# Convolution, product and store of the last inner tile of a gated FFN written into the first chunk of the down projection

## Chip, cores and metric

The kernel runs on one core of a Trainium2 chip. The metric is the device time of one execution in microseconds; the median of 3 runs of the kernel before is 2664.31 us (2664.18 to 2665.32). Engines: TensorE (PE) multiplies matrices, VectorE (DVE), ScalarE (ACT) and GpSimd (POOL) work on elements, and SyncE (SP) issues most of the DMAs.

## The reference, cut to what matters

A decoder trunk of two layers on 1024 prompt tokens and 64 sample tokens, width 1024, all in float32. Each layer ends in a convolutional FFN:

```python
def conv_ffn(x, buf, w_up, conv_w, conv_b, w_down):
    h = x @ w_up                                  # 1024 -> 2 * 2816
    hp = jnp.concatenate([buf, h], axis=1)        # two rows of state ahead
    hc = conv_b + conv_w[0] * hp[:, 0:seq_len]
    for tap in range(1, 3):
        hc = hc + conv_w[tap] * hp[:, tap:tap + seq_len]
    gate, val = jnp.split(hc, 2, axis=-1)
    out = (jax.nn.gelu(gate) * val) @ w_down      # 2816 -> 1024
    return out, hp[:, -2:]                        # the last two rows are outputs too
```

## The kernel before

Every matrix product is done in three passes on a high and a low part of both operands (`mm3`, L815 to L817): a split is one ACT copy (L150) for the high part and one DVE subtraction (L151) for the low part.

The up projection, `ffn_up`, walks over 22 inner tiles `f` of 128 channels. Each has a gate half (s=0) and a value half (s=1). `inputs(f)` loads and splits the weights; `first(f)` and `rest(f, s)` are the products, whose results land in two buffers `hb` of tag `acc`. `conv(f, s)` is one ACT scaling with bias (L1198), two DVE taps (L1200), two small POOL copies of the last rows into `cvo` (L1203, L1204), and for the gate a GELU on ACT (L1206). `outputs(f)` multiplies gate and value on DVE (L1211) and stores the result to `gd` in DRAM (L1212). For odd `f` it also transposes the four pieces of `cvo` on PE (L1218), copies them into an 18-row buffer `cr` of tag `gr` (L1220) and stores that (L1223, L1224).

The down projection, `Down` and `ffn_down`, reads `gd` back. Its steps are (chunk, token tile) pairs. Chunk 0 takes inner tiles 0 and 1 in plain form: 9 steps k=0 to 8, the sample tile first, each with 12 products (8 for the sample tile) of L1426, evacuated by ACT (L1431). Chunk 1 and the following ones take four inner tiles each and pairs of token tiles by Strassen's scheme of seven products; their operands are differences that POOL makes (L1306 for weights, L1368 to L1371 for gated rows), their results are added by DVE (L1437). `stage(k)` loads the gated rows of step k (L1350 in chunk 0, L1354 for the sample tile, L1363 in the later chunks) and splits them. In chunk 0, step k is staged up to two steps ahead, and after each step two of 14 pieces of chunk 1's weights are prepared (`dn.load(1, 2)`). In layer 1 the last chunk is of Strassen's form, in layer 0 it is plain. The gated rows of inner tile 21, the last, are read by the last chunk only.

Buffers come from rings with a tag: 14 of `acc`, 5 of `gr`, 2 of `xr`, 2 of `raw`. The rows of steps 2 and 3 lie in `xr`, those of the other steps of chunk 0 in `gr`.

The order on each engine is not the order of the text. When the kernel is built, a planner plays the program with durations of its own and gives an engine, whenever it comes free there, the earliest-written instruction whose inputs and buffer are ready. Each engine and each DMA queue then executes its list strictly in that order. So a step that is written later loses to everything written before it that is ready at the same time, but it fills a hole if nothing else is ready.

Of the kernel before, what the change touches and what calls it, by code (L numbers as in the profile page):

```python
# [37 lines left out]
NF = FF // P  # L38
# [35 lines left out]
def trunk_kernel(ctx, tc, I, O):  # L74
# [19 lines left out]
    def psum_t():  # L94
        return psum("tr")
# [708 lines left out]
    def slot(tag, shape=None, dtype=F32):  # L804

        al = {"gx": "acc", "post": "acc", "junk": "gr"}
        shp, bufs = {"acc": ([P, 2 + SEQ + NB * 10], NACC), "gx": ([P, 4, 2 * P], NACC), "gr": ([P, 512], NGR),
                     "xr": ([P, D], 2), "junk": ([P, D], NGR), "post": ([P, D], NACC),
                     "cvo": ([P, 4, 18], 2), "cpar": ([P, 2 * NF, 20], 1), "ss": ([P, 1], 4)}[tag]
        tag = al.get(tag, tag)  # L810
        return pools["ph"].tile(shape or shp, dtype, tag=tag, name=nm(tag), bufs=bufs)
# [10 lines left out]
    def row_bcast(src):  # L822
        t = slot("post")
        nc.sync.dma_start(t, src.partition_broadcast(P))
        return t
# [272 lines left out]
    def ffn_up(i, down):  # L1098
# [8 lines left out]
        def inputs(f):  # L1107
            raws, hbs = [], []
            for s in range(2):
                raw = pools["w"].tile([P, 1024], F32, tag="raw", name=nm("raw"), bufs=2)  # L1110
                rv = u3(raw)
                nc.sync.dma_start(rv, wv[:, :, s * FF + f * P : s * FF + (f + 1) * P])
                raws.append(rv)
            a11, a12, a21, a22 = [r[:, 4 * k : 4 * k + 4] for r in raws for k in range(2)]
            s12, s34 = u3(slot("xr")), u3(slot("xr"))
            s1, s2, s3, s4 = [t[:, 4 * k : 4 * k + 4] for t in (s12, s34) for k in range(2)]
            V.tensor_tensor(s1, a21, a22, ALU.add)
            V.tensor_tensor(s2, s1, a11, ALU.subtract)
            V.tensor_tensor(s3, a11, a21, ALU.subtract)
            V.tensor_tensor(s4, a12, s2, ALU.subtract)  # L1120
            ws = []
            for r in (raws[0], s12, s34, raws[1]):
                hi, lo = u3(wslot("whi", F32R)), u3(wslot("wlo", F32R))
                split_evac(hi, lo, r)
                ws.append((hi, lo))
            for s in range(2):
                hb = slot("acc")
                hs = hb[:, 2 + SEQ :].rearrange("p (b r) -> p b r", r=10)
                GP.memset(hb[:, 0:2], 0.0)
                GP.tensor_copy(hs[:, :, 0:2], cp[:, s * NF + f, 4:NPAR].rearrange("p (b r) -> p b r", r=2))  # L1130
                hbs.append(hb)
            st[f] = ws, hbs, []
# [12 lines left out]
        def first(f):  # L1145


            (wg, w12, w34, wv_), (hg, hv), _ = st[f]
            lo, hi = slice(2, 2 + HT), slice(2 + HT, 2 + 2 * HT)
            p1, p2, p3 = psum(), psum(), psum()  # L1150
            v1, v2, v3 = [t[:, 0:HT] for t in (p1, p2, p3)]
            m1, u2, u3_ = hv[:, lo], hg[:, hi], hv[:, hi]
            prod(p1, wg, 0, x(0, 0), True)
            A.copy(m1, v1)  # L1154
            if f < NAHEAD:
                prod(p1, wg, 4, x(4, 0), False)
                A.copy(hg[:, lo], v1)
                yield
            prod(p2, w12, 4, lambda k: cb.rhs(0, k), True)
            V.tensor_tensor(u2, v2, m1, ALU.add)  # L1160
            prod(p3, w12, 0, x(0, HT), True)
            prod(p2, w34, 0, lambda k: cb.rhs(1, k), False)
            V.tensor_tensor(u3_, v2, m1, ALU.add)
            V.tensor_tensor(u3_, v3, u3_, ALU.add)
            if f >= NAHEAD:
                prod(p1, wg, 4, x(4, 0), False)
                A.copy(hg[:, lo], v1)
            prod(p3, w34, 4, x(4, HT), False)
            V.tensor_tensor(u2, v3, u2, ALU.add)  # L1169
            yield  # L1170
            prod(p2, wv_, 4, lambda k: cb.rhs(2, k), False)
            V.tensor_tensor(m1, v2, m1, ALU.add)
            yield
# [15 lines left out]
        def conv(f, s):  # L1189
            _, hbs, hcs = st[f]  # L1190
            if s == 0 and f % 2 == 0:
                cvos[f] = slot("cvo")
            cvo = cvos[f - f % 2]
            ft = s * NF + f
            hb = hbs[s]
            hs = hb[:, 2 + SEQ :].rearrange("p (b r) -> p b r", r=10)
            hc = slot("acc")[:, 0:TG]
            A.activation(hc, hb[:, 2 : 2 + TG], AF.Identity, bias=cp[:, ft, 3:4], scale=cp[:, ft, 2:3])  # L1198
            for tap in (1, 0):
                V.scalar_tensor_tensor(hc, hb[:, tap : tap + TG], cp[:, ft, tap : tap + 1], hc,  # L1200
                                       op0=ALU.mult, op1=ALU.add)
            co = cvo[:, 2 * s + f % 2]
            GP.tensor_copy(co[:, 0:2], hb[:, SEQ : SEQ + 2])  # L1203
            GP.tensor_copy(co[:, 2:NCV].rearrange("p (b r) -> p b r", r=2), hs[:, :, 8:10])  # L1204
            if s == 0:
                A.activation(hc, hc, AF.Gelu_apprx_tanh)  # L1206
            hcs.append(hc)

        def outputs(f):
            hcs = st.pop(f)[2]  # L1210
            V.tensor_tensor(hcs[1], hcs[0], hcs[1], ALU.mult)  # L1211
            nc.sync.dma_start(gd[f, :, 0:TG], hcs[1])  # L1212
            if f % 2 == 1:

                cvo = cvos.pop(f - 1)
                ps = psum_t()
                for j in range(4):
                    PE.transpose(ps[0:NCV, j * P : (j + 1) * P], cvo[:, j], ident)  # L1218
                cr = slot("gr")
                A.copy(cr[0:NCV], ps[0:NCV])  # L1220
                crv = cr.rearrange("r (s f) -> r s f", s=2)
                fs = slice((f - 1) * P, (f + 1) * P)
                nc.sync.dma_start(O["conv_prompt"][i, 0].rearrange("r (s f) -> r s f", s=2)[:, :, fs], crv[0:2])  # L1223
                nc.sync.dma_start(O["conv_sample"][i].rearrange("b r (s f) -> (b r) s f", s=2)[:, :, fs],  # L1224
                                    crv[2:NCV])
# [13 lines left out]
        for f in range(NAHEAD, NF):  # L1239
            inputs(f)  # L1240
            if f == NF - 1:
                down.begin()
            for s, _ in enumerate(first(f)):
                rest(f, s)
                conv(f, s)
            outputs(f)
        tail.combos = None


# [131 lines left out]
    def ffn_down(dn, i, xsrc, xdst, norm):  # L1381
# [5 lines left out]
        def fetch(j):  # L1387

            if not norm and j <= NTT:
                tt = ORDER[j]  # L1390
                r = slot("xr") if j % 2 else pools["w"].tile([P, 1024], F32, tag="raw", name=nm("raw"), bufs=2)
                nc.sync.dma_start(r[0 : tokens(tt)[1]], xsrc(tt))
                res[tt] = r
# [107 lines left out]
        def finish():  # L1501
            while ends:
                done(ends.pop(0))

        for k, (c, tt) in enumerate(dn.steps):
            kind, f0, nf = dn.plan[c]
            if c == nch - 1 and post[0] is None:
                post[0] = row_bcast(I["f_post_g"][i])
                for j in range(4):
                    fetch(j)  # L1510
            if kind == "p":
                dn.upto(k + 2)
                plain(k, c, tt)
                flush()
                if c == 0:
                    dn.load(1, 2)
            elif tt == NTT:
                sample(k, c)
                flush()
                dn.upto(k + 1)  # L1520
                finish()
            else:
                last = tt == 6
                g = pair(k, c, tt)
                for j in range(7):
                    if j == 2:
                        flush()
                        dn.upto(k + 1)
                        if not (norm is False and last):
                            finish()  # L1530
                    next(g)
                    if last and j != 2:
                        dn.load(c + 1, 1)
                if not last:
                    dn.load(c + 1, 1 if norm and c == nch - 2 else (3, 2, 2)[tt // 2])
                rest.append((g, c + 1 if last else nch))
            if c == nch - 1:
                ends += [tt] if kind == "p" or tt == NTT else [tt, tt + 1]
                if kind == "p":
                    finish()  # L1540
# [528 lines left out]
    down = Down(0)  # L2069
# [8 lines left out]
    down = Down(1)  # L2078
# [34 lines left out]
```

## Time and profile before

| what | value |
|---|---|
| median of 3 runs | 2664.31 us |
| profiled execution | 2665.99 us, of which the span is 2664.1 us |
| PE / DVE / ACT / POOL busy | 94% / 73% / 48% / 25% of the span |
| share of PE on the chain that ended last | 58% |
| passage from up to down projection, layer 0 | about 930 to 990 us from the span's start |
| the same, layer 1 | about 2385 to 2445 us |

A row of a timeline gives start, duration, engine, line, operation, tiles written and read, and in brackets how long the engine stood idle before it and what ended that. A busy PE is not PE at its peak, since the durations of matmuls overlap; distances between starts are safer. The granted clock (PEclk) is 1.00 at full speed.

### The profile page before, as it was taken

How to read it: one execution, taken by the hardware profiler on the slowest of the kernel's cores; microseconds unless marked ns; L12 is line 12 of the kernel's file. 1: busy time of each engine (PE TensorE's matmuls, PEld its weight loads, DVE VectorE, ACT ScalarE, POOL GpSimd, SP SyncE). 2: the span in 40 equal slices, each digit the busy share in tenths (PEclk: the TensorE clock that was granted, in tenths of full speed). 3: DMA queues.
4: the chain of work that ended last, by engine and by line, in shares of the span. 5: the costliest groups of instructions: out<-in, count | busy, mean ns of one | idle time of the engine just before them, and what ended most of it. 6: DMA issues, size and time to landing. Idle time of an engine off the chain costs nothing.

```text
span 2664.1 us, 39516 instructions
## 1 busy us (share of the span) xinstructions
PE 2493.7 (94%) x14234; PEld 2199.5 (83%) x14234; DVE 1947.8 (73%) x3543; ACT 1281.0 (48%) x2597; POOL 661.2 (25%) x1062
## 2 busy tenths in 40 slices
PE   3778998999999999999999899999899999998997
PEld 2777876999999977788777788877799999996776
DVE  7994358677777789984222688875877777778999
ACT  6763234444444454354322677764544444444433
POOL 3220030111111176501201222113011111127571
PEclk9999998999999999999999899999899999999999
DMA  5443233122222233445646333325322222233334
GB/s 144 104 97 88 84 126 126 58 76 78 85 72 78 81 117 97 125 134 183 207 158 210 104 83 96 98 93 173 127 69 79 75 75 74 75 98 105 92 107 154
DMA packets 265688, 286.77 MB, mean 108 GB/s; under 512 B 42268, under 2 KB 212564, under 8 KB 265492
## 3 DMA queue, kind: packets, MB, share of 16 engines
q1 hardware_dynamic: 261892, 273.55, 33.3%
q0 software_dynamic: 3088, 9.77, 1.7%
q8 instruction: 113, 1.85, 0.3%
q10 hardware_dynamic: 512, 0.92, 0.1%
q14 instruction: 83, 0.68, 0.1%
HBM read 193.58 MB, written 70.93 MB: 99 GB/s over the span
## 4 chain that ended last, share of the span: by engine, by line
PE 58%; DVE 13%; DMA 4%; issue 4%; ACT 3%; POOL 3%; SPq 0%; DVEq 0%; ACTq 0%; POOLq 0%
PE mm L815 17%; PE mm L817 17%; PE mm L816 17%; DVE acc L1437 2%; PE mm L1426 2%; DVE xT_lo L151 2%; DMA gr<-gd 2%; DVE S L1907 1%; ACT S L1911 1%; DVE xT_hi L151 1%; DVE wst L151 1%; PE mm L1935 1%; PE tr L876 1%; DVE acc L860 1%; POOL xr L1306 1%
## 5 line engine op out<-in xcount | busy, mean ns | idle before, releaser
L815 PE MATMUL mm<-xT_hi,whi 128*128 128x384 f32 (+1 forms) x1408 | 457.0, 325 | 2.0 <-ACT acc L1154 1.7
L816 PE MATMUL mm<-xT_lo,whi 128*128 128x384 f32 (+1 forms) x1408 | 456.2, 324 | 1.4 <-DVE xT_lo L151 1.4
L817 PE MATMUL mm<-xT_hi,wlo 128*128 128x384 f32 (+1 forms) x1408 | 454.0, 324 | 0.0
L815 PEld LDWEIGHTS mm<-xT_hi,whi 128*128 128x128 f32 x1408 | 265.4, 189 | 3.8 <-ACT acc L1154 2.4
L816 PEld LDWEIGHTS mm<-xT_lo,whi 128*128 128x128 f32 x1408 | 265.7, 189 | 2.2 <-DVE xT_lo L151 2.1
L817 PEld LDWEIGHTS mm<-xT_hi,wlo 128*128 128x128 f32 x1408 | 265.3, 189 | 0.8
L1203 POOL COPY cvo<-acc 128x2 f32<-128x2 f32 x88 | 54.2, 616 | 814.1 <-ACT acc L1186 814.0
L815 PE MATMUL mm<-whi,xT_hi 128*128 128x512 f32 x608 | 242.9, 404 | 5.8 <-ACT whi L798 5.8
L1200 DVE SCALAR_TENSOR_TENSOR acc<-acc,cpar,acc 128x1104 f32<-128x1104 f32 x176 | 239.9, 1385 | 4.7 <-ACT acc L1198 4.7
L816 PE MATMUL mm<-wlo,xT_hi 128*128 128x512 f32 x608 | 242.8, 400 | 0.1
L817 PE MATMUL mm<-whi,xT_lo 128*128 128x512 f32 x608 | 242.2, 400 | 0.0
L150 ACT CAST whi<-raw 128x1024 fp32r<-128x1024 f32 x88 | 92.7, 1053 | 248.5 <-PE mm L817 245.1
L1437 DVE TENSOR_TENSOR acc<-mm,acc 128x512 f32<-128x512 f32 x279 | 184.3, 679 | 8.4 <-PE mm L817 8.1
L151 DVE TENSOR_TENSOR wlo<-raw,whi 128x1024 fp32r<-128x1024 f32 x88 | 107.7, 1224 | 103.5 <-PE mm L816 90.8
L815 PE MATMUL mm<-acc,whi 128*128 128x384 f32 x528 | 178.8, 339 | 2.5 <-DVE acc L1160 2.5
L817 PE MATMUL mm<-acc,wlo 128*128 128x384 f32 x528 | 178.9, 339 | 0.0
L816 PE MATMUL mm<-acc,whi 128*128 128x384 f32 x528 | 178.3, 338 | 0.0
L815 PEld LDWEIGHTS mm<-whi,xT_hi 128*128 128x128 f32 x608 | 115.3, 190 | 36.9 <-ACT whi L798 6.2
L816 PEld LDWEIGHTS mm<-wlo,xT_hi 128*128 128x128 f32 x608 | 115.2, 189 | 27.9 <-DVE wlo L799 0.8
L817 PEld LDWEIGHTS mm<-whi,xT_lo 128*128 128x128 f32 x608 | 114.9, 189 | 27.9 <-issue 0.8
L1198 ACT ACTIVATE acc<-acc,cpar 128x1104 f32<-128x1104 f32 x88 | 114.2, 1313 | 18.1 <-DVE acc L1169 11.9
L1186 ACT COPY acc<-mm 128x256 f32<-128x256 f32 x88 | 32.4, 369 | 183.7 <-PE mm L817 183.7
(575 smaller groups left out, 6311.6 us busy)
## 6 DMA issues: line engine op xcount, KB each, us to landing
raw<-in_w_up_dram SPq DMA_DIRECT2D x88, 512.0 KB
gd<-acc SPq DMA_DIRECT2D x44, 552.0 KB
raw<-in_w_down_dram SPq DMA_DIRECT2D x44, 512.0 KB
gr<-gd SPq DMA_DIRECT2D x80, 256.0 KB
raw<-in_glu_w_dram SPq DMA_DIRECT2D x40, 256.0 KB
acc<-in_cache_k_dram SPq DMA_DIRECT2D x16, 512.0 KB
acc<-in_cache_v_dram SPq DMA_DIRECT2D x16, 512.0 KB
xj<-in_x_prompt_dram SPq DMA_DIRECT2D x8, 512.0 KB
```

The source lines that it names most:

```text
L150: A.copy(hi_ap, ps_ap)
L151: V.tensor_tensor(lo_ap, ps_ap, hi_ap.bitcast(F32), ALU.subtract)
L815: PE.matmul(out, lh, rh, start=start, stop=False, **kw)
L816: PE.matmul(out, lh, rl, start=False, stop=False, **kw)
L817: PE.matmul(out, ll, rh, start=False, stop=stop, **kw)
L860: V.scalar_tensor_tensor(y[:, hs], y[:, hs], r[0:n], xr[0:n, hs], op0=ALU.mult, op1=ALU.add)
L1186: A.copy(hb[:, 2 + n0 : 2 + SEQ], ps[:, 0:wp])
L1198: A.activation(hc, hb[:, 2 : 2 + TG], AF.Identity, bias=cp[:, ft, 3:4], scale=cp[:, ft, 2:3])
L1200: V.scalar_tensor_tensor(hc, hb[:, tap : tap + TG], cp[:, ft, tap : tap + 1], hc, op0=ALU.mult, op1=ALU.add)
L1203: GP.tensor_copy(co[:, 0:2], hb[:, SEQ : SEQ + 2])
L1426: PE.matmul(pa[h], lt, wt[:, h * 512 : (h + 1) * 512], start=st and j == 0, stop=sp and j == len(seq) - 1)
L1437: V.tensor_tensor(a, ps, a, ALU.add)
```

## The change

`conv(21, 0)`, `conv(21, 1)` and `outputs(21)`, 21 being the last inner tile, are no longer called at the end of `ffn_up`. They are left in a list, and `ffn_down` calls one of them after each of the steps k=3, 4 and 5 of chunk 0, behind that step's two pieces of weights. Both layers are changed alike.

```diff
@@ -1242,8 +1242,12 @@
                 down.begin()
             for s, _ in enumerate(first(f)):
                 rest(f, s)
-                conv(f, s)
-            outputs(f)
+                if f < NF - 1:
+                    conv(f, s)
+            if f < NF - 1:
+                outputs(f)
+
+        down.left = [lambda: conv(NF - 1, 0), lambda: conv(NF - 1, 1), lambda: outputs(NF - 1)]
         tail.combos = None
 
@@ -1514,6 +1518,8 @@
                 flush()
                 if c == 0:
                     dn.load(1, 2)
+                    if k >= 3 and dn.left:
+                        dn.left.pop(0)()
             elif tt == NTT:
```

## Rows read from the trace of the kernel before

**Rows 1.** The page's busy times: engine, us, share of the span, instructions.
```profile
PE 2493.7 (94%) x14234; PEld 2199.5 (83%) x14234; DVE 1947.8 (73%) x3543; ACT 1281.0 (48%) x2597; POOL 661.2 (25%) x1062
```
**Rows 2.** Layer 0 by stretches: us, busy PE, PEld, DVE, ACT, POOL, clock, DMA.
```profile
940.00:950.00 10.00, 8.02 (x36) 6.08 (x34) 10.00 (x8) 8.47 (x14) 8.07 (x4) 1.00 0.37 111
950.00:960.00 10.00, 6.41 (x17) 4.79 (x18) 9.03 (x13) 3.67 (x9) 5.55 (x2) 0.72 0.58 185
960.00:970.00 10.00, 10.00 (x42) 8.01 (x41) 6.57 (x10) 7.08 (x17) 8.64 (x11) 0.94 0.24 75
970.00:980.00 10.00, 9.49 (x41) 7.14 (x39) 8.34 (x15) 7.88 (x19) 9.46 (x16) 1.00 0.49 135
980.00:990.00 10.00, 9.43 (x39) 6.94 (x39) 9.32 (x15) 2.07 (x5) 6.92 (x8) 1.00 0.37 116
...
1010.00:1050.00 40.00, 39.14 (x167) 30.84 (x166) 38.05 (x59) 14.54 (x32) 26.41 (x36) 1.00 0.33 93
```
**Rows 3.** PE's waits from 920 to 985: for whom, us in total, times, longest.
```profile
PE mm L1426 <- ACT xT_lo L150: 3.5, 1, 3.5
PE mm L1426 <- DVE xT_lo L151: 2.1, 1, 2.1
```
**Rows 4.** PE's timeline, layer 0: chunk 0 and the start of chunk 1.
```profile
937.47 0.71 PE L1426 MATMUL mm<-whi,gr 128*128 128x512 f32 x2
...
947.62 0.40 PE L1426 MATMUL mm<-whi,xT_lo 128*128 128x512 f32 x1
951.52 1.22 PE L1426 MATMUL mm<-whi,xT_lo 128*128 128x512 f32 x2 [3.50 <-ACT xT_lo L150]
...
957.05 1.39 PE L1426 MATMUL mm<-whi,xT_lo 128*128 128x512 f32 x4 [2.07 <-DVE xT_lo L151]
...
970.83 0.39 PE L815 MATMUL mm<-wst,xT_lo 128*128 128x512 f32 x1
```
**Rows 5.** PE's timeline, layer 1: first products of chunk 0 and of chunk 1.
```profile
2392.10 0.71 PE L1426 MATMUL mm<-whi,gr 128*128 128x512 f32 x2
...
2425.82 0.39 PE L815 MATMUL mm<-wst,xT_lo 128*128 128x512 f32 x1
```
**Rows 6.** ACT's timeline, layer 0: the GELU, and the splits behind it.
```profile
946.58 1.13 ACT L1206 ACTIVATE acc<-acc 128x1104 f32<-128x1104 f32 x1 [1.20 <-DVE acc L1200]
...
951.07 0.71 ACT L150 CAST xT_lo<-gr 128x256 fp32r<-128x256 f32 x2
```
**Rows 7.** DVE's timeline, layer 0: two taps, and the next splits of gated rows.
```profile
944.14 4.74 DVE L1200 SCALAR_TENSOR_TENSOR acc<-acc,cpar,acc 128x1104 f32<-128x1104 f32 x2
...
956.58 1.09 DVE L151 TENSOR_TENSOR xT_lo<-gr,xT_lo 128x256 fp32r<-128x256 f32 x3
```
**Rows 8.** SP's timeline, layer 0: issues of loads and stores.
```profile
940.02 2.68 SPq L1350 DMA_DIRECT2D gr<-gd  x4
...
954.10 0.68 SPq L1223 DMA_DIRECT2D out_conv_prompt_dram<-gr  x1
...
957.82 0.38 SPq L1350 DMA_DIRECT2D gr<-gd  x1
958.29 15.51 SPq L1363 DMA_DIRECT2D gr<-gd  x6
```
**Rows 9.** The taps' line in the whole run: ns shortest, median, longest.
```profile
L1200 DVE SCALAR_TENSOR_TENSOR acc<-acc,cpar,acc x176: 1350/1361/2423, 478.7 to 2406.8; 128x1104 f32<-128x1104 f32 x176
```
**Rows 10.** POOL's timeline, layer 0: differences for weights, then for gated rows.
```profile
945.34 2.37 POOL L1306 TENSOR_TENSOR xr<-raw,raw 128x512 f32<-128x512 f32 x1
...
954.37 4.44 POOL L1306 TENSOR_TENSOR xr<-raw 128x512 f32<-128x512 f32 x1 [4.37 <-DVE xT_hi L151]
...
962.94 0.91 POOL L1368 TENSOR_TENSOR gr<-gr 128x128 f32<-128x128 f32 x1
```
**Rows 11.** Layer 1, a later stretch of the down projection; columns as in rows 2.
```profile
2490.00:2540.00 50.00, 49.55 (x214) 39.63 (x213) 48.68 (x80) 19.00 (x43) 33.12 (x45) 1.00 0.36 105
```
**Rows 12.** PE's waits from 2440 to the end: for whom, total, times, longest.
```profile
PE mm L815 <- DVE acc L1437: 5.8, 6, 2.6
```

## The prediction

> **What bounds the kernel now.** I read the page's list of busy times first [rows 1]: TensorE (PE) is busy 94% of 2664.1 us and VectorE (DVE) 73%, so a gain has to come from time in which PE stands or runs slowly, and DVE is the next to be full. Then I went to the one place that the change touches, the passage from the up projection into the down projection, which occurs once per layer, and cut it into stretches of 10 us [rows 2]. In layer 0 the reader sees PE busy 8.02 and 6.41 of 10 us from 940 to 960, a granted clock of 0.72 in the second, while DVE is at 10.00 and 9.03. PE's waits [rows 3] name two: 3.5 us for ACT and 2.1 us for DVE, both for a split of gated rows into `xT_lo`. PE's own timeline [rows 4] puts them in chunk 0 of the down projection: its first product starts at 937.47, PE waits before 951.52 and before 957.05, and chunk 1 starts at 970.83 (L815).
>
> Chunk 0 has 104 products (8 for the sample tile, 12 for each of 8 tiles). From 937.47 to 947.62 there are 44 of them without a wait: 10.15 us over 43 steps, 0.236 us each. So 104 x 0.236 = 24.5 us would do; it took 970.83 - 937.47 = 33.4 us. **8.9 us are lost in layer 0**: 3.5 + 2.1 of waiting and about 3.3 of products at a lower clock behind the waits. In layer 1 chunk 0 runs from 2392.10 to 2425.82 [rows 5]: 33.7 us, so 9.2 are lost. Together 18.1 us: no gain at this place can be more.
>
> Why does PE wait? The products of 951.52 are step k=4 (8 + 3 x 12 = 44 products lie before). Its split on ACT stands at 951.07, behind the GELU of the last inner tile, which itself waited for DVE [rows 6]. DVE at that time does that tile's convolution: two taps from 944.14 that took 4.74 us, and only at 956.58 come the next splits of gated rows [rows 7]. The other half of the cause is on SP [rows 8]: the loads of steps 4 to 7 go out together at 940.02, and the loads of step 8 (957.82) and of chunk 1 (from 958.29) stand behind the stores of `outputs(21)` (954.10 and following).
>
> **The change, part by part.** No instruction is added or removed: per layer, two ACT scalings, one GELU, four DVE taps (L1200, median 1.361 us, longest 2.423 [rows 9]), one DVE product, four small POOL copies, four PE transposes with one ACT copy, and three stores on SP are written later, after steps 3, 4 and 5.
>
> *What leaves chunk 0's front.* The splits of steps 4 and 5 and eight pieces of chunk 1's weights are now written before the first tap and win where both are ready. Also, `cr`, the 18-row buffer of `outputs(21)`, is of tag `gr`, and the loads of steps 4 to 7 took their buffers from the same tag after it. That four loads left SP back to back [rows 8], with their buffers not all due at one moment, I read as a plan that had to place `cr` first. Now `cr` comes after step 7's buffer, so the loads of steps 4 to 7 should go out earlier. I take both waits of rows 3 as gone, with the slow clock behind them: -8.9 us at PE if nothing else is late. From the other side it may be 0, if the planner fills the same free DVE time with the taps as now; they are long ready by then.
>
> *What is late next: DVE.* The taps still have to be done before chunk 1 is in full flow. DVE's idle time from 940 to 990 is 0 + 0.97 + 3.43 + 1.66 + 0.68 = 6.7 us [rows 2]. Work that is only moved can pull the rest forward by no more than this. In chunks that run well DVE is still idle 1.95 of 40 us (1010 to 1050), 2.4 us in 50. So 6.7 - 2.4 = 4.3 us are to be had, not 8.9.
>
> *What is late next: chunk 1's loads.* Steps 8 and 9 now take their `gr` buffers after `cr`, whose copy needs the transposes, written behind step 5: (8 + 5 x 12) x 0.236 = 16.0 us after the start, 953.5, and about 1 us for the transposes and the copy. The loads of chunk 1 would go out near 955, some 3.5 us sooner than at 958.29. From that load to chunk 1's first product it is 970.83 - 958.29 = 12.5 us now; if all of that is needed the start comes at 967.5, a gain of 3.3; if a part of it is slack, DVE's 4.3 decides. POOL has its share in these 12.5 us: it does differences for weights until 962.94 and only then the four differences of the first staged piece, of which the first took 0.91 us [rows 10].
>
> *The moved queues.* On SP the store of `gd` and the two of `cr` move past the loads of steps 4 to 7, a gain, and stay ahead of those of chunk 1. On ACT the GELU stays ahead of the evacuations of some later step of chunk 0; ACT waited 1.20 us at it [rows 6] and may again. On PE the transposes stand among the products; in the run before they cost no wait that the view of waits shows. The store of `gd` for f=21 is read by the last chunk only, far away. I set all this at 0, bounded by 1.2 either way per layer from the GELU's wait.
>
> *The port.* Two taps took 4.74 us, 2.37 each [rows 7], where the median is 1.361 [rows 9], while POOL worked on differences, of which one took 2.37 us [rows 10]: about 1.0 us lost by each tap. Of the four taps of this tile I see two paying it. Moved on, all four can: POOL is busy 8.64 and 9.46 of 10 us from 960 to 980 [rows 2], 5.55 and 8.07 earlier. That is 2 x 1.0 us more on DVE at most and 2 x 1.0 us less if none meets it; I take 0.
> The Trainium skill (SBUF — State Buffer, section "SBUF: two separate sides") speaks against the change here: VectorE operations with two SBUF inputs and GpSimd operations share a port pair that is locked for a whole instruction, and the other side blocks. The two rows of 2.37 us agree. By that rule alone every moved tap could hold POOL up for its full length, which would delay chunk 1 rather than start it earlier; that is the last rival below, priced there from rows: by the rule its 2672, by the rows the sum below.
>
> *Sum.* Layer 0: 8.9 from the waits, cut to 4.3 by DVE and to 3.3 to 4.3 by chunk 1's loads; I take 4. Layer 1 has the same geometry, but there DVE is busy 48.68 of 50 us further on [rows 11], and PE waits 5.8 us in all for its additions into `acc` [rows 12]; what is won at the start can partly be lost there. I take 3. Together 7 us. The profiled execution took 2665.99 us (its span of 2664.1 and 1.9 around it): 2665.99 - 7 = 2659.0. It lay 1.7 us above the median of 2664.31, so against that median **2657.3 us**.
>
> **The rivals.** What a measurement of this kernel tells from no change is about 0.2%, 5.3 us.
>
> *All of it is won (2646 to 2652).* If DVE's work gets shorter too, because taps no longer meet POOL (up to 2 us per layer) and the splits come in time, 12 to 18 us go. For it: the waits are plainly behind the taps. Against: DVE's 6.7 us of idle per passage.
>
> *Nothing happens (within 4 us, 2660 to 2668).* The planner hands DVE whatever is ready; the taps are ready soon after 940 and the weights' pieces wait for POOL (its difference of 2.37 us ends at 947.7 [rows 10]), so the taps would fall into the same hole as now. For it: from 940 to 950 DVE has no idle time, so whatever is ready runs. Against: the loads' order on SP should move all the same.
>
> *Slower (about 2672).* The mechanism is POOL's chain of differences for chunk 1, held up by the moved taps. Four taps of 1.36 us put in POOL's way are 5.4 us, and chunk 1's second product needs that chain. It decides from the point at which chunk 1's first L815 comes later than 33.4 us after the first L1426. With 1.4 us for the first product (6 x 0.236) as the only cover, chunk 1 is 4 us later in each layer: 2664.3 + 8 = 2672. For it: POOL at 8.64 and 9.46 of 10 us. Against: chunk 0 frees POOL's 4.37 us wait for DVE [rows 10] when weights are split sooner.
>
> **Chances.** The forecast (2653 to 2660.5, both layers gain 2 to 6 us) 0.46; all of it 0.10; nothing 0.24; slower 0.20. Of the forecast about 0.08 lies above 2659, within 0.2%, and the case of nothing lies there whole. That gives faster 0.38 + 0.10 = 0.48, same 0.08 + 0.24 = 0.32, slower 0.20. The range runs from 2648 (half of the case in which all is won) to 2670 (most of the case of nothing, a part of the slower one); the forecast's own range is 2653 to 2660.5.
>
> **What would show it.** In the changed profile: the loads L1350 of steps 4 to 7 issued before 940 relative to the same start (first L1426 at 937.5); no wait of PE before the 45th product; the granted clock at 1.00 through chunk 0; L1200 no longer between 944 and 952 but after the split of step 5; chunk 1's first L815 29 to 30 us after the first L1426 in both layers, and DVE idle under 4 us in the 50 us from the start of the passage. The prediction is wrong if the taps stand where they stood, if the loads of step 8 and chunk 1 come later than 20 us after the first L1426, or if a PE wait of more than 4 us shows up at chunk 1's first products on a POOL difference.

## The result and the profile after

The changed kernel takes 2675.58 us, median of 7 runs (2670.93 to 2680.25); the kernel before, beside it, 2664.31 us (2661.79 to 2668.01, 7 runs). The ratio is 1.0046, with a 95% interval of 1.0037 to 1.0056: the change makes the kernel **slower by 11.3 us**, where 2657.3 was forecast and 2670 was the end of the range. The profiled execution took 2676.99 us, its span 2675.2. Lines are shifted by four in the changed kernel: the plain products are L1430, ACT's evacuation L1435, DVE's additions into `acc` L1441, the loads of plain steps L1354, those of Strassen steps L1367.

The page's busy times, answering to [rows 1]: PE is busy 5 us less, DVE 10.5 us more, POOL 37 us less. (31.6 of POOL's 37 lie between the attention and chunk 0 of layer 1, in small copies that take less long; that stretch as a whole is 0.7 us longer.)
```profile
PE 2488.4 (93%) x14234; PEld 2194.6 (82%) x14234; DVE 1958.3 (73%) x3543; ACT 1278.3 (48%) x2597; POOL 624.1 (23%) x1062
```

**Chunk 0 did move.** PE's timeline in layer 0, answering to [rows 4], and in layer 1, to [rows 5]:
```profile
934.22 0.63 PE L1430 MATMUL mm<-whi,gr 128*128 128x512 f32 x2
...
958.86 1.75 PE L1430 MATMUL mm<-whi,xT_lo 128*128 128x512 f32 x4 [4.38 <-DVE xT_lo L151]
...
965.16 0.40 PE L815 MATMUL mm<-wst,xT_lo 128*128 128x512 f32 x1
...
2398.66 0.62 PE L1430 MATMUL mm<-whi,gr 128*128 128x512 f32 x2
...
2432.35 0.39 PE L815 MATMUL mm<-wst,xT_lo 128*128 128x512 f32 x1
```
The two waits of [rows 3] are gone from layer 0, and one of 4.38 us stands in a later step. Chunk 0 takes 965.16 - 934.22 = 30.9 us where it took 33.4; in layer 1 it takes 33.7 as before. The start itself is 3.3 us earlier than in the profile before, though the text up to there is the same; the twelve further kernels with that text start between 932.6 and 936.7, so that this is chance.

SP shows the loads early, as forecast (answers to [rows 8]):
```profile
897.03 4.28 SPq L1354 DMA_DIRECT2D gr<-gd  x3
...
928.79 0.38 SPq L1354 DMA_DIRECT2D gr<-gd  x1
...
939.36 0.38 SPq L1354 DMA_DIRECT2D gr<-gd  x1
944.52 0.33 SPq L1296 DMA_DIRECT2D raw<-in_w_down_dram  x1
944.94 0.67 SPq L1223 DMA_DIRECT2D out_conv_prompt_dram<-gr  x1
...
947.72 15.48 SPq L1367 DMA_DIRECT2D gr<-gd  x4
```
Three of the four loads that left together at 940.02 before, 2.6 us after chunk 0's start, now leave from 897.03 on, 37 us ahead of it. The last load of a step of chunk 0 leaves 5.1 us after chunk 0's start (before: 957.82 - 937.47 = 20.4 us), the first of chunk 1 at 13.5 (before 20.8).

**Where the time went.** On DVE, answering to [rows 7], the taps stand behind more splits, but in front of those that step 7 needs:
```profile
948.89 5.78 DVE L1200 SCALAR_TENSOR_TENSOR acc<-acc,cpar,acc 128x1104 f32<-128x1104 f32 x3 [0.26 <-ACT acc L1198]
954.59 1.74 DVE L151 TENSOR_TENSOR xT_lo<-raw,xT_lo 128x512 fp32r<-128x512 f32 x1
956.26 2.55 DVE L151 TENSOR_TENSOR xT_lo<-gr,xT_lo 128x256 fp32r<-128x256 f32 x3
```
Three taps take 1.93 us each on average, where the median is 1.361 [rows 9]; the split behind them takes 1.74 us, where the shortest of that size take 0.68. The taps are no longer than they were: all four take 7.3 us, before 7.5. What has grown is the splits. The windows of 50 us from the first product of chunk 0 (busy PE, PEld, DVE, ACT, POOL, then clock and DMA as in [rows 2]), first of the kernel before, then of the changed one:
```profile
937.47:987.47 50.00, 43.35 (x171) 33.01 (x169) 43.84 (x57) 30.57 (x66) 38.31 (x41) 0.93 0.44 134
```
```profile
934.22:984.22 50.00, 42.55 (x176) 32.54 (x175) 48.76 (x55) 31.24 (x64) 42.89 (x44) 0.97 0.40 122
```
This pair is the heart of the case. DVE's idle time fell from 6.2 to 1.2 us, as I had wanted it to, and DVE got through 55 instructions in place of 57. The idle time was filled by longer instructions (0.89 us each for 0.77): at the short length of each line and shape (5th percentile of both profiles) those that start in the 50 us would take 34.4 us, before 35.5, and what they take above it rose from 11.9 to 17.1. The clock rose as forecast from 0.93 to 0.97, and PE came only 3 products further (176 matmuls for 171, of which 4 and 1 are transposes).

Stretches that answer to those of [rows 2]:
```profile
950.00:960.00 10.00, 5.62 (x23) 3.94 (x22) 9.96 (x8) 7.46 (x15) 8.67 (x7) 0.96 0.14 43
960.00:970.00 10.00, 9.50 (x36) 7.28 (x34) 10.00 (x14) 6.46 (x15) 9.61 (x14) 0.87 0.41 134
970.00:980.00 10.00, 8.87 (x36) 6.61 (x36) 10.00 (x14) 3.39 (x8) 9.38 (x12) 1.00 0.60 175
...
1010.00:1050.00 40.00, 36.64 (x156) 28.82 (x155) 38.61 (x58) 13.18 (x30) 24.45 (x34) 1.00 0.28 84
```
From 960 to 980 DVE is at 10.00, where it had 6.57 and 8.34, and even from 1010 to 1050 PE makes 156 products where it made 167, at the full clock.

What chunk 0 won is lost again in chunks 1 to 4. PE's waits there in layer 0 (971 to 1142, and 965 to 1142), before and after:
```profile
PE mm L815 <- DVE acc L1437: 1.3, 3, 0.5
```
```profile
PE mm L815 <- DVE acc L1441: 8.7, 8, 1.9
```
In layer 1, from 2446 to the end, where [rows 12] has 5.8 us:
```profile
PE mm L815 <- DVE acc L1441: 10.1, 10, 2.6
```
PE waits until DVE has added an earlier product into `acc`. The additions themselves are no longer than before (0.676 us for 0.678 on average in layer 1); they come late, behind splits in DVE's list that are long. That the splits' length is the reason is put to the test in experiment 3.

Cut at the same products in every trace, the spans differ by these stretches (us; "excess" is my own working: over all DVE instructions from chunk 0 to the last chunk's first product in layer 0, to the end in layer 1, the time above the short ones, the 5th percentile, of the same line and shape):

| stretch | before | after | difference |
|---|---|---|---|
| start to chunk 0, layer 0 | 937.5 | 934.2 | -3.3 |
| layer 0: chunk 0 | 33.4 | 30.9 | -2.5 |
| layer 0: chunk 1 to the last plain chunk's end | 228.6 | 234.0 | +5.4 |
| layer 1, first part of the attention | 540.8 | 541.7 | +0.9 |
| end of the attention and start of its output projection (PE's instructions 9490 to 9890) | 79.5 | 84.7 | +5.2 |
| from there to chunk 0, layer 1 | 572.4 | 573.1 | +0.7 |
| layer 1: chunk 0 | 33.7 | 33.7 | 0.0 |
| layer 1: chunk 1 to the end | 238.3 | 242.9 | +4.6 |
| excess of DVE, layer 0 / layer 1 | 31.9 / 40.2 | 36.4 / 44.3 | +4.5 / +4.1 |

These are single executions, and the traces of the experiments below show how far they scatter. Where layer 0 is that of before (nine traces), the way from chunk 0 to the last plain chunk's end takes 260.9 to 262.4 us with an excess of 30.5 to 32.1. Where layer 1's text is that of before and POOL makes its differences (four traces), chunk 0 to the end takes 272.0 to 273.9 us with an excess of 39.7 to 40.2. Against that, layer 0's 264.9 us and its excess are clear of the scatter; of layer 1's 4.6 us it is 2.7.

Two things were to be explained: the loss behind chunk 0, and 5.2 us in the attention of layer 1, which the change does not touch.

### The profile page after: what moved, and what is told of

The parts are those of the page before. It is cut to its first block, busy times and chain, and to the rows that moved or that the text cites. A ratio compares the mean times of both kernels' runs of the same rounds, so it can differ in the third digit from the quotient of the medians.

```text
span 2675.2 us, 39551 instructions
## 1 busy us (share of the span) xinstructions
PE 2488.4 (93%) x14234; PEld 2194.6 (82%) x14234; DVE 1958.3 (73%) x3543; ACT 1278.3 (48%) x2597; POOL 624.1 (23%) x1062
## 5 line engine op out<-in xcount | busy, mean ns | idle before, releaser
L1203 POOL COPY cvo<-acc 128x2 f32<-128x2 f32 x88 | 48.2, 547 | 837.2 <-ACT acc L1186 837.2
L150 ACT CAST whi<-raw 128x1024 fp32r<-128x1024 f32 x88 | 92.4, 1050 | 280.5 <-PE mm L817 275.7
L1441 DVE TENSOR_TENSOR acc<-mm,acc 128x512 f32<-128x512 f32 x279 | 183.6, 677 | 9.0 <-PE mm L817 8.1
L817 PEld LDWEIGHTS mm<-whi,xT_lo 128*128 128x128 f32 x608 | 114.2, 188 | 27.5 <-issue 0.9
L1913 DVE CUSTOM_DVE_ANT_0 S<-mm,tb 128x512 f32<-128x512 f32 (+3 forms) x192 | 101.2, 551 | 21.0 <-PE mm L1911 17.5
```

Of the source, the lines that this page charges most:

```text
L150: A.copy(hi_ap, ps_ap)
L817: PE.matmul(out, ll, rh, start=False, stop=stop, **kw)
L1441: V.tensor_tensor(a, ps, a, ALU.add)
L1913: V.tensor_tensor_reduce(S_[j][:, k0 : k0 + w], ps[:, 0:w], H["tb"][:, b0 : b0 + w], 0.125, -3e38, ALU.add, ALU.max, mx[:, j, c : c + 1])
```

## The experiments

The theories, as the expectations name them: A, collisions of DVE's instructions with POOL's in the passages, and a new order of the lists at the end of the attention; B, that the loss in the attention is chance; C, that the earlier loads do the damage; D, that the moved work itself does; E, that the lists play no part; F, that POOL's work is too long, whatever it does. Medians stand beside those of the kernel before on the same chip.

**1. One layer at a time.** In `ffn_up` the tile is left over in one layer alone (`i != 1` for the other kernel):
```diff
-                if f < NF - 1:
+                if f < NF - 1 or i != 0:
                     conv(f, s)
-            if f < NF - 1:
+            if f < NF - 1 or i != 0:
                 outputs(f)
-        down.left = [...]
+        down.left = [...] if i == 0 else []
```


> The change in layer 0 alone. Theory A (each passage loses by itself, because moved taps make DVE's splits collide with POOL; and a change in layer 0 also makes the planner order the end of attention and the output projection anew): about +2.6 us in layer 0's passage and down projection, +6 us between 1725 and 1830 us, nothing in layer 1: +8 to +9 us in all, ratio 1.003. Theory B (what was lost near 1725 to 1830 is chance from run to run): +2 to +3 us, ratio 1.001. If the forecast holds in a layer by itself: -4 us.

Layer 0 alone: 2672.42 us against 2664.18, ratio 1.0031 (1.0020 to 1.0043), so +8.2 us.

> The change in layer 1 alone; the list of every engine is that of the kernel before up to layer 1's passage. Theory A: +4 us, all of it behind the first product of layer 1's chunk 0, nothing at the end of attention; ratio 1.0015. Theory B: the same +4, with the 6 us at the end of attention there or not by chance. If the forecast holds in a layer by itself: -3 us.

Layer 1 alone: 2666.77, ratio 1.0011 (1.0002 to 1.0020), +2.6 us; I had expected 4. The two add up to 10.8 of the 11.3 us. Layer 0's change carries most of it, and more than its own stretch shows: with layer 0 alone changed, that down projection (from chunk 0 to the last plain chunk's end) takes 263.0 us, where it took 262.0 before, and the attention's end 84.7 us again, where the kernel with layer 1 alone changed has 81.7. DVE's excess there is 34.0 us, with the same lists as in the changed kernel, which had 36.4. With layer 1 alone changed, layer 1's down projection takes 273.4 us with an excess of 40.4: no more than the unchanged ones. The traces thus do not show where the 2.6 us of layer 1 lie.

**2. The two halves of the change, in layer 1.** First only the 18-row buffer `cr`, its transposes and stores put off, so that the loads go out early while the taps stay; then only convolution, GELU, product and store of `gd` put off, so that the loads stay late:
```diff
+            if f < NF - 1 or i == 0:
+                last_rows(f)
+
+        def last_rows(f):
             if f % 2 == 1:
...
+        down.left = [lambda: None, lambda: None, lambda: last_rows(NF - 1)] if i == 1 else []
```


> Layer 1 alone; convolution, product and the store of gated rows stay where they were, only the transposes, the copy into the 18-row buffer and its two stores move behind step 5. Theory A (the buffer's place sets when the loads of steps 4 to 7 go out, the taps' place sets DVE's collisions): loads go out early, PE's first wait in chunk 0 shrinks, taps stay: 0 to -4 us. Rival C (early loads are what does the damage, since early splits crowd DVE before chunk 1): +2 to +4 us as with the whole change.

2663.72 us, ratio 0.9996 (0.9987 to 1.0005): no difference. The loads of steps 4 to 7 went out early, chunk 0 took 31.4 us, the whole down projection 271.3 (272.0 to 273.9 where it is unchanged). Early loads of chunk 0 do no harm, so C falls for them; they also win next to nothing. The first load of chunk 1 stayed at 20.9 us after chunk 0's start (before 20.0), so this run does not clear those.
```diff
-                conv(f, s)
-            outputs(f)
+                if f < NF - 1 or i == 0:
+                    conv(f, s)
+                else:
+                    rows(f, s)
+            if f < NF - 1 or i == 0:
+                outputs(f)
+            else:
+                last_rows(f)
+        down.left = [lambda: conv(NF - 1, 0), lambda: conv(NF - 1, 1), lambda: outputs(NF - 1)] if i == 1 else []
```


> Layer 1 alone; taps, GELU, product and the store of gated rows move, the last rows' copies, transposes and stores stay. Theory A: loads of steps 4 to 7 go out as before, so PE's wait in chunk 0 stays, and DVE's taps collide later: +3 to +6 us. Rival C: about 0.

2666.27 us, ratio 1.0007 (0.9998 to 1.0016). Against my expectation chunk 0 shrank, to 28.9 us, though the loads of steps 4 to 7 were late; the first of chunk 1 left at 13.5 us. The rest grew from 238.3 to 245.2. So the taps' place makes about half of chunk 0's loss of 9.2 us, and all of that gain is paid for behind it (274.1 us in all, 272.0 to 273.9 unchanged): PE's waits for additions from chunk 1 to the end come to 10.7 us in 11 places.

**3. POOL without its reads.** In layer 1's down projection POOL writes a constant where it made a difference:
```diff
+            self.diff = (lambda o, a, b, op: GP.memset(o, 0.01)) if i else GP.tensor_tensor
-                        GP.tensor_tensor(v[n], v[dif[n][0]], v[dif[n][1]], ALU.subtract)
+                        self.diff(v[n], v[dif[n][0]], v[dif[n][1]], ALU.subtract)
```
and the same for the four sums of gated rows. This once with the text's order of before, once with the taps of layer 1 put off, and once with the whole change in layer 1.

> Kernel before, but in layer 1's down projection POOL writes a constant where it formed differences of weights and of gated rows (these differences are left out), so POOL reads nothing from SBUF there. Control for the next one. Theory A (DVE's lengthened operations come from POOL's reads on the shared port): what DVE's operations in layer 1's passage and down projection take above their short durations falls from 38.8 us to under 10, and the stretch from chunk 0's first product to the end from 272.0 to 260 us or less. Rival D (DVE's durations vary for another reason, and DVE's plain work is the bound): excess stays above 25 us, the stretch within 4 us of 272.

> The same constants on POOL in layer 1, with the taps, GELU, product and store of layer 1's last inner tile moved and the last rows' part left in place. With POOL reading, that move shortened chunk 0 by 4.8 us and lost 6.9 us behind it. Theory A: without POOL's reads the gain of chunk 0 is kept or there is no loss to give back: 0 to 5 us shorter than the control. Rival D: chunk 1 and later still lose, 1 to 3 us longer than the control.

> The change in layer 1 as it is (all three calls behind steps 3 to 5), with constants written by POOL in layer 1's down projection in place of its differences (left out), to be held against the control without the change (stretch from chunk 0 to the end 253.8 us there, 272.0 and 273.4 to 276.6 with POOL's reads). Theory A (POOL's reads on the shared port make both the wait that the change was to remove and the loss behind it): 252 to 255 us, DVE's excess under 6 us, no difference to the control within 0.1%. Rival D (the moved work itself is what costs): 256 us or more.

Text of before: 2646.93 us, ratio 0.9940 (0.9922 to 0.9957). Taps put off: 2646.58, 0.9932 (0.9917 to 0.9947). Whole change: 2643.16, 0.9918 (0.9904 to 0.9933). Layer 1 takes 253.8, 253.2 and 253.4 us from chunk 0 to the end, for 272.0: some 18 us are gone, and with them the difference that the change makes there: the moved work by itself costs nothing, once POOL reads nothing, and D falls. PE's timeline of the first of the three:
```profile
2386.57 0.71 PE L1427 MATMUL mm<-whi,gr 128*128 128x512 f32 x2
...
2411.60 0.40 PE L815 MATMUL mm<-wst,xT_lo 128*128 128x512 f32 x1
```
Chunk 0 takes 25.0 us with the taps where they were in the text: about the 24.5 that I had worked out for a chunk without a wait. DVE's groups of the down projection in layer 1 (count, then busy us and mean ns of one, then its idle time before them), before:
```profile
L1437 DVE TENSOR_TENSOR acc<-mm,acc 128x512 f32<-128x512 f32 x155 | 102.3, 678 | 2.9 <-PE mm L817 2.9
L151 DVE TENSOR_TENSOR xT_lo<-gr,xT_lo 128x256 fp32r<-128x256 f32 (+2 forms) x53 | 34.5, 660 | 4.6 <-ACT xT_lo L150 3.0 <-PE mm L1426 1.4
```
after:
```profile
L151 DVE TENSOR_TENSOR xT_lo<-gr,xT_lo 128x256 fp32r<-128x256 f32 (+2 forms) x52 | 36.1, 708 | 3.3 <-ACT xT_lo L150 3.2
```
and with the text's order of before but POOL writing constants:
```profile
L1438 DVE TENSOR_TENSOR acc<-mm,acc 128x512 f32<-128x512 f32 x155 | 103.9, 687 | 18.8 <-PE mm L817 17.0 <-PE mm L1446 1.5
L151 DVE TENSOR_TENSOR xT_lo<-gr,xT_lo 128x256 fp32r<-128x256 f32 (+2 forms) x53 | 23.8, 461 | 6.5 <-ACT xT_lo L150 6.2
```
The same 53 splits take 461 ns for 660. DVE's excess in the stretch, 40.2 us by the definition above (38.8 in the expectation), falls to 3.8, and DVE, no longer late, now waits 17.0 us for PE before its additions. The additions stay as long as they were: one of their operands is a product in PSUM (`mm`), only the other lies in SBUF.

A constant is also written faster than a difference (POOL had 43 us of work in place of 159), so POOL's length was a rival. To tell the two apart, each constant was written three times:
```diff
-            self.diff = (lambda o, a, b, op: GP.memset(o, 0.01)) if i else GP.tensor_tensor
+            self.diff = (lambda o, a, b, op: [GP.memset(o, 0.01) for _ in range(3)]) if i else GP.tensor_tensor
```


> The kernel before, but in layer 1's down projection POOL writes a constant three times over where it made a difference (the differences are left out). In the run with one constant each POOL had 42.7 us of such work in that stretch (160 of 205 ns, 34 of 527 ns), against 159 us of differences; three each give 128 us, 3 x 205 = 615 ns where a difference of gated rows took 609 to 626. So POOL's chain is nearly as long as before, but reads nothing from SBUF. Theory A (what costs is that POOL's differences read SBUF beside DVE's splits): the stretch from layer 1's chunk 0 to the end stays at 253 to 257 us, the median at 2644 to 2651, and the splits into xT_lo at some 0.46 us. Rival F (what costs is POOL's length: chunk 1's operands come later, whatever POOL does meanwhile): the stretch goes back to 264 to 272 us, the median to 2657 to 2665, while the splits stay short.

2646.47 us against 2665.14, ratio 0.9932 (0.9909 to 0.9956); the stretch takes 253.2 us and chunk 0 24.4. A window of layer 1 in that trace, answering to [rows 11]:
```profile
2490.00:2540.00 50.00, 50.00 (x217) 40.47 (x216) 45.66 (x87) 22.51 (x49) 31.25 (x156) 1.00 0.39 110
```
POOL is busy 31.25 of 50 us, nearly the 33.12 of before, and PE stands at 50.00 all the same. F falls: it is not how long POOL works, but what it reads while DVE works. Two differences to the real kernel remain in all four. A constant does not wait for the load of its operands. And the planner, which plays the constants too, writes other lists: 101 of the 416 rows of DVE's list in that stretch stand elsewhere than before, and the taps run at 1.2 to 8.7 us after chunk 0's start where they ran at 3.5 to 14.7. The shorter splits are measured by themselves; how much of the 18 us comes from them and how much from these two is not shown. Layer 0, which carries most of the loss, had no such run.

**4. Layer 0's tile later or sooner.** The condition `k >= 3` in `ffn_down` becomes `k >= 6` or `k >= 1`, with layer 0 alone changed:
```diff
-                    if k >= 3 and dn.left:
+                    if k >= 6 and dn.left:
```


> Layer 0 alone, the three calls behind steps 6, 7 and 8 instead of 3, 4 and 5. In this version the planner's lists from the end of attention on are those of the kernel before. Theory A (the new lists there cost about 5 us): +1 to +4 us, from layer 0's passage alone, with 79 to 83 us for the end of attention. Theory B (that stretch varies by chance): the same as layer 0's change behind steps 3 to 5, +8.

> Layer 0 alone, the three calls behind steps 1, 2 and 3. Here the lists of layer 0's passage differ least from those of the kernel before, but those from the end of attention on are the other ones, as in the changed kernel. Theory A: +4 to +7 us, nearly all between the end of attention and the output projection. Theory B: 0 to +2 us.

With 6: 2666.86 us against 2664.96, ratio 1.0004 (0.9993 to 1.0014). With 1: 2670.49, 1.0020 (1.0011 to 1.0029). The planner's lists may explain the order of the two medians; the two profiled executions, at 2670.77 and 2669.64 us, do not show it. Compared row by row, the lists for layer 1's attention are those of before with 6, and are others with 1, as they are with 3: between the two down projections DVE's list differs at 267 places, 51 of them in this stretch, under a text that is the same. The stretch took 78.0 to 83.3 us in the eleven traces with the lists of before (mean 81.5) and 84.7, 84.7 and 87.1 in the three with the new lists (mean 85.5). That is 4.0 us, with no overlap, and E falls with it. With 1, layer 0's own down projection is the shortest of all, 259.5 us; the 5.6 us over the mean in the attention eat that up.

B is right for a part of the 5.2 us, and POOL and DVE show it at the start of the stretch, where the lists are still the same. Before, DVE's combination (L1921, starting at 1741.20) was ahead of POOL's subtraction, and POOL took the longer time:
```profile
1741.20 1.14 DVE L1921 SCALAR_TENSOR_TENSOR S<-S,cc,S 128x896 f32<-128x896 f32 x1
```
```profile
1741.78 2.81 POOL L1879 TENSOR_TENSOR kl<-qraw,kl 128x1024 fp32r<-128x1024 f32 x1 [5.21 <-ACT kl L1878]
```
After, POOL is ahead, and DVE takes 2.90 us for the same combination (L1927):
```profile
1742.84 2.90 DVE L1927 SCALAR_TENSOR_TENSOR S<-S,cc,S 128x896 f32<-128x896 f32 x1
```
```profile
1742.40 2.40 POOL L1885 TENSOR_TENSOR kl<-qraw,kl 128x1024 fp32r<-128x1024 f32 x1 [7.02 <-ACT kl L1884]
```
DVE ends when POOL has ended and its own 1 us is done (1742.40 + 2.40 + 0.94 = 1745.74). Which of the two starts first is not the change's doing: with the lists of before, DVE is first in three traces, where the stretch takes 78.0 to 79.6 us, and POOL is first in eight, where DVE takes 2.9 us and the stretch 81.3 to 83.3 (mean 82.4). The profile before is one of the three. With the new lists POOL is first in all three traces. So about 3 us (85.5 for 82.4) go with the new lists, and the rest of the 5.2 is who came first. What in the new lists costs the 3 us I have not shown.

**5. Both layers late, and layer 1 early.** The same condition with 6 in both layers, and with 1 in layer 1 alone:

> Both layers, the three calls behind steps 6 to 8 in place of 3 to 5; the lists between the layers are those of the kernel before. Theory A: chunk 0 shorter still (27 to 29 us), chunk 1 and later longer by more than that, +2 to +3 us in each layer, nothing at the end of attention: +3 to +6 us, about half of what the change cost. Rival E (the loss is set by how far the moved work gets into chunk 1, and the planner's lists elsewhere do not matter): +10 us or more.

> Layer 1 alone, the three calls behind steps 1 to 3: taps before most of chunk 0's later splits, the loads of steps 5 and later behind the 18-row buffer. In layer 0 this place gave 259.5 us from chunk 0's first product to the end of the last products, 2.5 less than before. Theory A (only the number of collisions counts): -2 to +1 us; if it is below the kernel before by its interval it is the version to take.

Both with 6: 2669.10 us against 2664.54, ratio 1.0016 (1.0007 to 1.0024), with the lists of before in the attention. Its chunk 0 takes 27.5 and 27.8 us, shorter by 5.9 and 6.0; the rest is longer, by 6.9 in layer 0 and by 9.8 in layer 1. Layer 1 alone with 1: 2661.88, ratio 0.9991 (0.9982 to 1.0000). That is the best of all, 2.7 us, at the edge of what the runs tell from nothing; its down projection took 269.4 us where it took 272.0.

Put side by side, layer 0 gives a series in the place of the tile (chunk 0, then chunks 1 to 4, up to the last chunk's first product, us): before 33.4 and 171.3; from k = 1 32.2 and 168.6; from k = 3 30.6 and 174.9 (layer 0 alone) or 30.9 and 176.5 (both); from k = 6 27.4 and 179.2 (layer 0 alone) or 27.5 and 178.1 (both). From 1 to 6 the later the tile comes, the shorter is chunk 0 and the longer what follows; from 1 to 3 that is longer by more, from 3 to 6 by more in one pair of traces (4.3 for 3.1 us) and by less in the other (1.6 for 3.4). The excess does not follow the place: 34.5 us with 1, 34.0 and 36.4 with 3, 33.5 and 33.8 with 6.

## Why the prediction was wrong

**Right:** that PE's waits in chunk 0 were to be had at all, and their size (24.5 us for a free chunk 0; 24.4 to 25.0 were measured in three of the four kernels of experiment 3; in the other, chunk 1's first products stand among those of chunk 0); that `cr` held back the loads, which did go out early; that DVE's idle time would fall below 4 us in the 50 us (1.2). **Half right:** the wait before the 45th product went, but another came in step 7; the clock of the second stretch rose from 0.72 to 0.96, not to 1.00, and sank to 0.87 in the third; chunk 1 came 30.9 us after chunk 0's start in layer 0, not 29 to 30, and in layer 1 it gained nothing.

**Wrong, the step that failed:** "So 6.7 - 2.4 = 4.3 us are to be had", with the term of the port set at 0. I took DVE's idle time as room into which work can be pulled forward, each instruction at its length of before. The idle time went, and it was filled by instructions that had become longer: 55 in 48.76 us for 57 in 43.84. The excess of DVE grew by 4.5 us in layer 0 and 4.1 in layer 1, and the waits for additions by 8.7 - 1.3 = 7.4 and 10.1 - 5.8 = 4.3 us. For the four taps the 0 was right, and the bound of 2 us held (7.3 us for 7.5 in layer 0, 6.6 for 7.5 in layer 1). But the splits of chunks 0 to 4 also stand beside POOL's differences, and for those the sum had no term; it ended at chunk 1's start, and for layer 0 counted what was won there as kept. In this pair of profiles the missing term is the 4 to 5 us of excess; with one layer changed alone it was 2 to 4 us in layer 0 (34.0 against 30.5 to 32.1) and nearly none in layer 1 (40.4 against 39.7 to 40.2), so that its size stays open. None of the prediction's three signs of being wrong showed: they all looked at chunk 0 and the start of chunk 1, and the loss came behind.

**Half wrong, the cause of the wait:** I read the waits as the taps' place in DVE's list. Their place is half of it (28.9 us when only taps, GELU and product moved). But with POOL's reads gone the taps may stay where they are in the text, and chunk 0 takes 25.0 us. The reading that fits is that the list was too long because its instructions were; since the planner's list changed too in that run, it is argued and not shown alone.

**Not seen:** that a change in layer 0 can re-order lists some 800 us later, in text that is the same. The prediction holds no term for it; it goes with some 3 to 4 of the 11.3 us. I had named the planner as what decides, but thought only of the queues beside the change.

**The rivals.** The slower one, 2672, was nearest in size, and its ground, the shared port, was right. Its mechanism was not: it decides, as written, from a chunk 1 that starts later than 33.4 us after chunk 0, and that came at 30.9 and 33.7; no wait of PE on a difference of POOL's shows there. What was held up was DVE by POOL, not POOL by DVE. "Nothing happens" falls with the moved loads and waits.

The Trainium skill (SBUF — State Buffer, section "SBUF: two separate sides") says that a VectorE operation with two SBUF inputs takes the pair of ports that it shares with GpSimd as a lock for the whole instruction, and only against a GpSimd operation that reads SBUF. These runs agree in both parts: splits fall from 660 to 461 ns when POOL only writes, additions with one SBUF input stay at 678 to 687 ns, and it makes no difference whether POOL writes for 43 us or for 127 (73.6 + 53.4, from the groups of that trace). I had weighed the rule for the moved taps and for POOL's delay; I should have priced DVE's.

What stays open: what turns the excess into lost time behind chunk 0. In layer 1 the loss needs POOL's reads, since without them it is gone. But the sum of the excess does not set the time: with k = 1 in layer 0 it is 34.5 us in the shortest passage of all (259.5 us), with k = 3 34.0 in a longer one (263.0). Which splits are lengthened, and what waits for them, probably counts. That freed splits meet POOL's differences more often once DVE has no idle time left is argued, not shown. A rival that no run clears by itself is the loads of chunk 1, which left early both in the changed kernel (13.5 us after chunk 0's start, before 20.8) and with the taps alone put off (13.5); with POOL writing constants and the whole change they left at 8.6 us, and nothing was lost. Nor is it shown what layer 1's 4.6 us in the changed kernel come from, since with layer 1 alone changed its down projection took 273.4 us, within the 272.0 to 273.9 of the unchanged ones.

## What to carry to other kernels

Idle time on an engine is room only if the work that fills it keeps its length: before moving work on VectorE, compare the mean of its two-SBUF-input groups with their shortest instruction, and treat the difference as the first thing to remove, here some 18 us in one layer, in a kernel that leaves POOL's differences out, against the 2.5 that chunk 0 won by a better order. One profile of each kernel does not carry differences of 1 to 3 us: several kernels with the same stretch tell its scatter. Where a planner writes the lists, compare the order of the whole program after any edit, not only beside it, and try the same edit at several places, since one place can cost 8 us and another 2. To test a suspected collision, leave one engine its time but take away what it reads.

## What the runs showed of the hardware

POOL's writes alone do not slow VectorE: with POOL busy 31.25 of 50 us on constants, the 53 splits of gated rows on DVE took 460 ns on average, and 461 with POOL busy 11.30 of 50. And in a collision the side that starts second loses most of the time that the two share: DVE's combination at 1742.84 lost 1.76 us (2.90 for 1.14) of the 1.96 up to POOL's end, POOL's subtraction at 1741.78 lost 0.41 (2.81 for 2.40) of the 0.56 up to DVE's end. The same pair comes in all fourteen traces: DVE second in eleven, at about 2.89 us, and POOL second in three, at 2.81.
